# Local attention in a fused decoder layer: values two blocks behind the scores, with a fourth tile of probabilities

## Chip, core and metric

One core of a Trainium2 chip runs the whole layer as one program. The metric is device time in microseconds (us), the median over several executions; lower is better. The engines are called PE (TensorE, its products), PEld (TensorE's loading of weights), DVE (VectorE), ACT (ScalarE), POOL (GpSimd) and SP (SyncE, which here only issues DMAs).

## What is computed

The layer takes 1024 prompt tokens and 8 single decode tokens of width 1024 through one projection, three branches (a gated linear recurrence "a", local attention "s", attention into a memory of 256 tokens "c"), a gated merge, an output product, a norm, a gated feed-forward and a second norm. The change lies in the prompt's local attention: 16 query heads share 4 key/value heads of width 64, each block of 128 queries looks at its own block of keys and the one before, and a learned sink per head joins the softmax.

```python
def swa_prompt(q, k, v, sinks):
    nb = T // WINDOW                      # 8 blocks of 128
    s = jnp.einsum('bnqkgd,bnmkd->bnkgqm', qb, kband).astype(jnp.float32) * scale
    mask = (band[None] & real)[None, :, None, None]
    p = sink_softmax(s, mask, sinks).astype(v.dtype)
    o = jnp.einsum('bnkgqm,bnmkd->bnqkgd', p, vband)
    return o.reshape(B, T, Q_W)
```

The result of the branch is then multiplied by its own weight matrix and a gate and added to the merged sum, as those of the other two branches are: `merged = sum(gates[:, :, n] * (br @ w_branch[n]) ...)`.

## The kernel before

All values are float32. A float32 product is made of several products of a shortened form: every operand is split into a high part (a cast on ACT, line 79) and the rest (a subtraction on DVE, line 80), and `mm3` (lines 108 to 115) issues three products per pair, high by high, high by rest, rest by high.

The program goes through the projection (`project`), the memory attention (`mem_attention`), the local attention (`windows`), the last branch product, the output product, the feed-forward and the two norms. Intermediates that don't fit on the chip go to scratch in DRAM and come back.

The local attention is a stage of 32 blocks: 4 key/value heads (`kv`), and for each 8 blocks of 128 queries (`b`). A block has two steps.

- `win_scores` (lines 556 to 590): 8 products of queries with keys into two PSUM banks of tag "s" (lines 574 and 575, four pairs); on DVE the mask is added and the maximum taken (line 578, four times), which writes the tile of probabilities `bp`; POOL copies the sinks into that tile (line 568); ACT takes the exponentials in place with their sums (line 582, four times); DVE takes the reciprocals (line 583); the four heads are scaled in place, one on DVE, one on POOL (line 589) and two on ACT (line 587).
- `win_values` (lines 592 to 612): 8 transposes of the probabilities on PE (line 599, four per block of keys, into banks of tag "t"), each group of four cast and subtracted into a high and a low part (`bph` on ACT, `bpl` on DVE), then two products with the values per block of keys into the one bank of tag "o" (lines 604 and 605), and two rounds of copy (ACT, line 609), sum (DVE, line 610) and store to scratch by SP (line 612). The first block of each head has one block of keys: half the transposes and products.

The tile `bp` has 4 heads by 257 columns, 4112 bytes in each partition, and tag "p" has three of them. `win_load` (lines 538 to 554) brings keys, queries and values of the next head by SP; it is called at block 4.

Between the two steps stand pieces of other work: `fill(1)` takes one step of the generators of branches a and c (`branch` and `product`, lines 633 to 663). A step is one chunk of 258, 386 or 388 tokens by 128 outputs: 24 products on PE, sometimes preceded by a load and a split of the next weights. Memory attention and local attention share these 48 steps; `build` (lines 1317 to 1330) runs what is left, after the first loads of branch s.

What sets the order of the instructions: the Python text gives each instruction a place, and a scheduler at compile time then gives each engine its own fixed order. It takes instructions whose operands are expected to be ready first, by the text's order among those, and an allocation of a tile waits for the readers of the tile that held the buffer before. So an engine's order can differ from the text. On the chip each engine runs its list in order and waits on semaphores.

Of the kernel before, what the change touches and what calls it, by code (L numbers as in the profile page):

```python
# [10 lines left out]
F32 = mybir.dt.float32  # L11
# [7 lines left out]
P = 128  # L19
# [37 lines left out]
class Builder:  # L57
# [498 lines left out]
    def win_scores(self, kv, ops, b):  # L556

        nc = self.nc
        nk = 2 if b else 1
        n = nk * P  # L560
        k0 = max(b - 1, 0) * P
        msk = self.mask[:, 256 - n:]
        ks, q, _ = ops
        snk = self.nsnk[:, 4 * kv:4 * kv + 4]
        st = self.sm.tile([P, 12], F32, tag="bst", name=f"bst{kv}_{b}", bufs=4)
        p = self.ph.tile([P, 4, 257], F32, tag="p", name=f"bp{kv}_{b}", bufs=3)
        pg = [p[:, g, :n] for g in range(4)]
        nc.gpsimd.tensor_copy(p[:, :, n], snk)
        for pr in range(2):
            s = self.bank("s", f"bs{kv}_{b}_{pr}")  # L570
            for u in range(2):
                qq = q[2 * pr + u][:, b * P:(b + 1) * P]
                o = s[:, u * 256:u * 256 + n]
                nc.tensor.matmul(o, qq, ks[0][:, k0:k0 + n], start=True, stop=False)
                nc.tensor.matmul(o, qq, ks[1][:, k0:k0 + n], start=False, stop=True)
            for u in range(2):
                g = 2 * pr + u
                nc.vector.tensor_tensor_reduce(pg[g], s[:, u * 256:u * 256 + n], msk, 1.0, snk[:, g:g + 1],  # L578
                                               ALU.add, ALU.min, st[:, g:g + 1])
        for g in range(4):  # L580
            x = p[:, g, :n + 1]
            nc.scalar.activation(x, x, AF.Exp, bias=st[:, g:g + 1], scale=-1.0, accum_out=st[:, 4 + g:5 + g])  # L582
        nc.vector.reciprocal(st[:, 8:12], st[:, 4:8])
        for g in range(4):
            r = st[:, 8 + g:9 + g]
            if g % 2:
                nc.scalar.mul(pg[g], pg[g], r)
            else:
                (nc.gpsimd if g else nc.vector).tensor_scalar_mul(pg[g], pg[g], r)
        return pg  # L590
# [23 lines left out]
    def windows(self, fill):  # L614

        self.mask = self.ph.tile([P, 256], F32, tag="mask", name="mask", bufs=1)
        self.nc.sync.dma_start(self.mask, self.io["cst"][:, P:P + 256])
        nxt, last = self.win_load(0), None
        fill(2)
        for kv in range(4):  # L620
            ops = nxt
            for b in range(8):
                pg = self.win_scores(kv, ops, b)
                if last:
                    fill(1)
                    self.win_values(*last)
                last = kv, ops, b, pg
                if b == 4 and kv < 3:
                    nxt = self.win_load(kv + 1)
        fill(1)  # L630
        self.win_values(*last)

    def product(self, step, br, m, c, wb, gate):

# [866 lines left out]
```

## Time and profile before

| what | value |
|---|---|
| median of 3 runs | 1961.04 us (1960.61 to 1963.18) |
| the profiled execution | 1959.34 us, its span 1957.5 us |
| granted clock of TensorE, mean | 0.996 |
| busy share of the span | PE 98%, PEld 96%, DVE 70%, ACT 52%, POOL 6% |
| the local attention's first product of scores, last sum | 833.3 us, 1045.1 us from the span's start |

The profile is of one execution. Busy time of an engine is the time in which an instruction of it was running; matmuls are pipelined, their ends are modelled, and consecutive ones overlap in the records, so a start-to-start distance tells more of a product's cost than its duration. A line of waits reads "who <- what it waited for: us in total, times, longest". A line of a window reads: the stretch, its length, then for each engine the busy time and in brackets the number of instructions, then the granted clock, the share of DMA and GB/s.

### The profile page before, as it was taken

How to read it: one execution, taken by the hardware profiler on the slowest of the kernel's cores; microseconds unless marked ns; L12 is line 12 of the kernel's file. 1: busy time of each engine (PE TensorE's matmuls, PEld its weight loads, DVE VectorE, ACT ScalarE, POOL GpSimd, SP SyncE). 2: the span in 40 equal slices, each digit the busy share in tenths (PEclk: the TensorE clock that was granted, in tenths of full speed). 3: DMA queues.
4: the chain of work that ended last, by engine and by line, in shares of the span. 5: the costliest groups of instructions: out<-in, count | busy, mean ns of one | idle time of the engine just before them, and what ended most of it. 6: DMA issues, size and time to landing. Idle time of an engine off the chain costs nothing. (4 is left out here: it accounts for less than half of the span.)

```text
span 1957.5 us, 37935 instructions
## 1 busy us (share of the span) xinstructions
PE 1917.8 (98%) x14356; PEld 1888.3 (96%) x14356; DVE 1362.4 (70%) x2875; ACT 1014.3 (52%) x2198; POOL 124.9 (6%) x202
## 2 busy tenths in 40 slices
PE   8999999999999899999999999999999999999997
PEld 8999999999999899989999999999999999999997
DVE  8678987887876645379877457976565655747566
ACT  5465565464666545388775245643333333635445
POOL 0000010010000000012110000000000000402001
PEclk9999999999999899999999999999999999999999
DMA  7444455455323776567535341122222222846554
GB/s 230 149 165 155 163 175 181 128 200 174 133 95 120 238 248 210 155 170 221 154 85 166 104 144 42 49 71 97 78 87 87 87 82 71 284 127 187 154 154 143
DMA packets 172199, 281.92 MB, mean 144 GB/s; under 512 B 20864, under 2 KB 87504, under 8 KB 171984
## 3 DMA queue, kind: packets, MB, share of 16 engines
q1 hardware_dynamic: 168144, 267.87, 43.6%
q0 software_dynamic: 3872, 11.63, 1.8%
q8 instruction: 112, 1.84, 0.4%
q14 instruction: 71, 0.58, 0.1%
HBM read 214.64 MB, written 66.85 MB: 144 GB/s over the span
## 5 line engine op out<-in xcount | busy, mean ns | idle before, releaser
L1229 PE MATMUL dl<-gh,wd_l 128*128 128x388 f32 (+2 forms) x528 | 168.9, 320 | 2.1 <-DVE wd_l L80 2.1
L1227 PE MATMUL dl<-gh,wd_h 128*128 128x388 f32 (+2 forms) x528 | 169.0, 321 | 1.1 <-ACT gh L79 1.1
L1228 PE MATMUL dl<-gl,wd_h 128*128 128x388 f32 (+2 forms) x528 | 168.7, 320 | 0.0
L1229 PEld LDWEIGHTS dl<-gh,wd_l 128*128 128x128 f32 x528 | 99.7, 189 | 2.5 <-DVE wd_l L80 2.5
L1227 PEld LDWEIGHTS dl<-gh,wd_h 128*128 128x128 f32 x528 | 99.5, 189 | 1.3 <-ACT gh L79 1.3
L1228 PEld LDWEIGHTS dl<-gl,wd_h 128*128 128x128 f32 x528 | 99.7, 189 | 0.5 <-DVE gl L80 0.5
L1236 POOL DMA_DIRECT2D gl<-scr_f x66 | 35.6, 544 | 795.1 <-PE fb L1163 637.5
L79 ACT CAST u_2h<-us 128x512 fp32r<-128x512 f32 x48 | 29.8, 621 | 87.4 <-PE ub L293 41.6
L79 ACT CAST u_1h<-us 128x512 fp32r<-128x512 f32 x48 | 29.8, 621 | 85.5 <-PE uc L293 37.4
L582 ACT ACTIVATE bp<-bp,bst 128x257 f32<-128x257 f32 (+1 forms) x128 | 62.8, 493 | 17.4 <-DVE bst L578 17.4
L276 DVE TENSOR_TENSOR us<-ur,ur 128x512 f32<-128x512 f32 x96 | 66.0, 687 | 5.8 <-DMA ur<-win 3.1
L276 DVE TENSOR_TENSOR us<-us,ur 128x512 f32<-128x512 f32 x96 | 66.1, 689 | 2.3
L80 DVE TENSOR_TENSOR u_4l<-us,u_4h 128x512 fp32r<-128x512 f32 x48 | 33.8, 705 | 44.5 <-PE fb L1163 29.9
L292 PE MATMUL ub<-th,u_6h 128*128 128x258 f32 x224 | 63.5, 283 | 0.0
L293 PE MATMUL ub<-tl,u_4h 128*128 128x258 f32 x224 | 63.4, 283 | 0.0
L293 PE MATMUL ud<-tl,u_1h 128*128 128x258 f32 x224 | 63.4, 283 | 0.0
L293 PE MATMUL ub<-tl,u_6h 128*128 128x258 f32 x224 | 63.4, 283 | 0.0
L293 PE MATMUL ub<-tl,u_2h 128*128 128x258 f32 x224 | 63.4, 283 | 0.0
L292 PE MATMUL ud<-th,u_1h 128*128 128x258 f32 x224 | 63.4, 283 | 0.0
L292 PE MATMUL ub<-th,u_4h 128*128 128x258 f32 x224 | 63.3, 283 | 0.0
L292 PE MATMUL ub<-th,u_2h 128*128 128x258 f32 x224 | 63.3, 283 | 0.0
L294 PE MATMUL ub<-th,u_4l 128*128 128x258 f32 x224 | 63.3, 283 | 0.0
(2718 smaller groups left out, 7917.7 us busy)
## 6 DMA issues: line engine op xcount, KB each, us to landing
ur<-win SPq DMA_DIRECT2D x112, 256.0 KB, 3.2
ur<-wgu SPq DMA_DIRECT2D x80, 256.0 KB, 2.7
scr_f<-ft SPq DMA_DIRECT2D x40, 258.0 KB, 3.1
dck<-cmk SPq DMA_DIRECT2D x32, 256.0 KB, 3.5
dcv<-cmvT SPq DMA_DIRECT2D x32, 256.0 KB, 2.8
st<-scr_q SPq DMA_DIRECT2D x32, 256.0 KB, 6.3
scr_g<-za SPq DMA_DIRECT2D x10, 516.0 KB, 3.8
scr_g<-zb SPq DMA_DIRECT2D x10, 516.0 KB, 2.6
```

Source lines behind the costliest of these rows:

```text
L79: ins = self.nc.scalar.copy(hi, src).ins
L80: self.nc.vector.tensor_sub(lo, src, hi.bitcast(F32))
L276: nc.vector.tensor_add(src, a, b)
L292: mm(sh[:, w], xh, start=opens and k == 0, stop=False)
L293: mm(sh[:, w], xl, start=False, stop=False)
L294: self.last_mm = mm(sl[:, w], xh, start=False, stop=k == 3).ins
L582: nc.scalar.activation(x, x, AF.Exp, bias=st[:, g:g + 1], scale=-1.0, accum_out=st[:, 4 + g:5 + g])
L1227: nc.tensor.matmul(ps, sh, mh, start=k == 0, stop=False)
L1228: nc.tensor.matmul(ps, sh, ml, start=False, stop=False)
L1229: self.last_mm = nc.tensor.matmul(ps, sl, mh, start=False, stop=closes and k == NF - 1).ins
L1236: self.nc.gpsimd.dma_start(lo.bitcast(F32), self.scf[f][:, t0:t0 + n])
```

## The change

The values of a block are taken from a queue of blocks whose scores are issued; before, the queue held one block, now it holds two. In the text, the scores of block n+2 (counted through all 32) now stand ahead of the filling step and the values of block n; before, those of block n+1 did. At the end two blocks are left and are emptied with one filling step each, so that the number of filling steps in the stage stays 34. The tag of the probabilities gets a fourth tile. Nothing else is changed, and no arithmetic.

```diff
-        p = self.ph.tile([P, 4, 257], F32, tag="p", name=f"bp{kv}_{b}", bufs=3)
+        p = self.ph.tile([P, 4, 257], F32, tag="p", name=f"bp{kv}_{b}", bufs=4)
...
-        nxt, last = self.win_load(0), None
+        nxt, late = self.win_load(0), deque()
         fill(2)
         for kv in range(4):
             ops = nxt
             for b in range(8):
                 pg = self.win_scores(kv, ops, b)
-                if last:
+                late.append((kv, ops, b, pg))
+                if len(late) > 2:
                     fill(1)
-                    self.win_values(*last)
-                last = kv, ops, b, pg
+                    self.win_values(*late.popleft())
                 if b == 4 and kv < 3:
                     nxt = self.win_load(kv + 1)
-        fill(1)
-        self.win_values(*last)
+        while late:
+            fill(1)
+            self.win_values(*late.popleft())
```

## The prediction, made before the changed kernel ran

> **What bounds the kernel now.** I read the page first, then windows over the stage, then its waits, then single tiles and the timeline.
>
> ```profile
> span 1957.5 us, 37935 instructions
> ...
> PE 1917.8 (98%) x14356; PEld 1888.3 (96%) x14356; DVE 1362.4 (70%) x2875; ACT 1014.3 (52%) x2198; POOL 124.9 (6%) x202
> ```
>
> PE is busy for 98% of the span, so time goes only where PE stands still. The local attention runs from about 833 to 1046 us. Its windows (the whole in the last row):
>
> ```profile
> core 0: us, PE busy (x) PEld busy (x) DVE busy (x) ACT busy (x) POOL busy (x), PEclk, DMA share, GB/s
> 833.00:850.00 17.00, 17.00 (x122) 16.41 (x121) 10.53 (x45) 10.12 (x35) 2.28 (x5) 1.00 0.58 140
> 850.00:875.00 25.00, 23.59 (x151) 20.27 (x150) 22.55 (x74) 24.57 (x74) 6.22 (x11) 1.00 0.63 173
> 950.00:975.00 25.00, 24.65 (x169) 23.22 (x167) 20.75 (x63) 19.22 (x59) 5.85 (x8) 1.00 0.41 125
> 1050.00:1060.00 10.00, 9.17 (x51) 8.87 (x52) 8.59 (x18) 7.21 (x15) 0.00 (x0) 1.00 0.97 322
> 833.00:1046.00 213.00, 209.82 (x1350) 194.41 (x1349) 175.20 (x540) 162.94 (x488) 40.98 (x61) 1.00 0.55 150
> ```
>
> Over 213 us PE is idle for 213 − 209.82 = 3.2 us at full granted clock. DVE (82%) and ACT (76%) have room on the whole; only from 850 to 875 is ACT full (24.57 of 25), and there PE loses 25 − 23.59 = 1.41 us, against 0.35 in the steady stretch from 950. The change adds and removes no product, so 3.2 us of PE idle, 0.16% of the time, is about all that a better order could win by this measure.
>
> The Trainium skill (Perfetto Trace Analysis, Identifying the Most-Contended Engine) holds matmul busy time for a poor measure of headroom and asks for the busy share of weight loads. By it the stage has 213 − 194.41 = 18.6 us of room instead of 3.2. The trace agrees only in part:
>
> ```profile
> L605 PE MATMUL bo<-bpl,vs 128*128 128x512 f32 x60 | 24.3, 404 | 0.0
> ...
> L605 PEld LDWEIGHTS bo<-bpl,vs 128*128 128x128 f32 x60 | 11.3, 188 | 1.2 <-DVE bpl L80 0.3
> ```
>
> Here a load takes 188 ns and stands idle behind a longer stream, with PE never idle before it (0.0). I keep PE's own idle time as the measure and use PEld's as the outer bound.
>
> **What waits for the probabilities now.** The change can only shorten waits of the transposes (L599), the first readers of `bp`. The tile of transposed probabilities, `bt`, and the stage's waits:
>
> ```profile
> L599 PEld LDWEIGHTS bt<-ident,bp x240: 137/140/144, 844.8 to 1041.2; 128*128 128x128 f32 x120
> ...
> L599 PEldq EVENT_SEMAPHORE  x8: 51/51/51, 844.8 to 869.5; - x8
> ...
>   ACT bp L587: 0.7, 3
> ```
>
> ```profile
> PEld bo L604 <- ACT bph L79: 7.6, 25, 0.6
> ...
> PE bo L604 <- ACT bph L79: 1.5, 7, 0.4
> ...
> POOL bp L568 <- PE bt L599: 18.7, 15, 3.6
> ```
>
> In 240 transposes PE waited three times for `bp`, 0.7 us in all. The separate semaphore waits ahead of transposes end at 869.5. What PE's loads do wait for, 25 times and 7.6 us, is the cast `bph` (L79), which follows the transposes inside the same step: the distance between scores and values doesn't touch it. The wait for a free `bp` tile exists, but on POOL, busy for 41 of 213 us.
>
> Why is there no more? I counted instructions finished at 960.5 us, just after the transposes that start at 959.77.
>
> ```profile
> 0.00:960.50 960.50, 23.00 (x84) 15.88 (x84) 0.99 0.55 175
> ```
>
> ```profile
> 0.00:960.50 960.50, 21.48 (x147) 17.47 (x148) 0.99 0.55 175
> ```
>
> ```profile
> 0.00:960.50 960.50, 8.60 (x21) 21.08 (x21) 0.99 0.55 175
> ```
>
> These are lines L574, L599 and L589. 84 scores at four a block are blocks 0 to 20. 148 transposes are blocks 0 to 19 (eight each, four in blocks 0, 8 and 16). The 21 scalings on DVE and on POOL say that block 20's probabilities are finished. The timeline then shows PE, and POOL's scaling of block 20:
>
> ```profile
> 959.77 1.04 PE L599 MATMUL bt<-ident,bp 128*128 128x128 f32 x8
> 960.56 0.36 PE L574 MATMUL bs<-ks,st 128*128 128x256 f32 x1
> 960.77 0.28 PE L575 MATMUL bs<-ks,st 128*128 128x256 f32 x1
> 961.05 0.49 PE L604 MATMUL bo<-bph,vs 128*128 128x512 f32 x1
> ...
> 962.55 0.34 PE L113 MATMUL brc<-HL0h,wbc_h 128*128 128x386 f32 x1
> ...
> 967.01 1.04 PE L599 MATMUL bt<-ident,bp 128*128 128x128 f32 x8
> ```
>
> ```profile
> 959.22 1.08 POOL L589 TENSOR_SCALAR bp<-bp,bst 128x256 f32<-128x256 f32 x1 [4.92 <-DVE bst L583]
> ```
>
> Block 20's probabilities are done at 959.22 + 1.08 = 960.30 and transposed at 967.01: they lie ready for 6.7 us. And the scores at 960.56, between block 19's transposes and its values, are block 21's. The scheduled order is two blocks ahead already, although the text says one; the third tile is what it uses for that. The change makes it three ahead of something that already waits for nothing.
>
> **The change part by part.** The sequence of fills and values is the same 34 fills and 32 blocks in the same order; what moves is the scores, one block up against it.
>
> *Work.* Per block, 8 products, 4 reductions, 4 exponentials, the reciprocal, 4 scalings and POOL's copy are issued earlier, none added: 0 us of PE work. What hides the softmax is one period of about 7 us now and about two after; it was hidden before. Gain: the 0.7 us of waits for `bp`, next to come late being the cast before L604, which is there already.
>
> *The wait for a tile.* POOL's copy of block n+4, where n+3 stood, waits for the transposes of n; behind it on POOL stand scalings of earlier blocks. As the old wait did (18.7 us over 15), it falls into POOL's idle time: 0 us, and without that cover one copy's wait, up to 3.6 us (the longest).
>
> *Queues.* The two stores per block stay with the values. `win_load` moves up one fill and one block of values on SP. Its queries need two tiles that the last scores of the head release; the queue's own waits have it:
>
> ```profile
> SPq L612 <- DVE bob L610: 27.2, 13, 4.8
> ...
> SPq L550 <- PE bs L575: 1.8, 3, 1.2
> ```
>
> That wait is 1.8 us in three times, far below the 27.2 us in which the same queue stands for the stores, and the scores that end it move with the loads. Between 0 and ±1.8 us; I take 0, as the loads have one more block of other work before their values are read.
>
> *Start and end.* Three score blocks instead of two stand ahead of the first fill in the text; PE is full there (17.00 of 17). At the end the first product of branch s comes with PE idle for 10 − 9.17 = 0.83 us. It hangs on the last block's stores, whose place doesn't change: 0.
>
> *The tile.* 4112 bytes more per partition, over memory that earlier tiles hold. The tile's first writer and the first scores:
>
> ```profile
> L568 POOL COPY bp<-nsnk x32: 188/228/1377, 813.1 to 1022.1; 128x4 f32<-128x4 f32 x32
> ```
>
> ```profile
> L574 PE MATMUL bs<-ks,st x128: 218/282/368, 833.3 to 1030.3; 128*128 128x256 f32 x112, 128*128 128x128 f32 x16
> ```
>
> POOL writes the first tile at 813.1, 20 us ahead of the first scores; the fourth takes memory of the stage before, too, and that would have to come free 20 us later to be felt. Cost 0.
>
> **The sum.** 0.7 us from the profiled execution's 1959.34 (span 1957.5 plus 1.84 around it) gives 1958.6; the median stands 1.70 above that execution, so 1960.3. A change of 0.2%, 3.9 us, is about what a measurement of this kernel can tell from none; smaller counts as the same.
>
> **The rivals.**
>
> *Nothing moves*: the scheduler, already ahead of the text, finds the same order in the steady part. 1961.0. Against it: the fourth tile is a real freedom.
>
> *The early stretch relaxes.* In 850 to 875 ACT is full, and transposes follow their scalings closely. With more distance, PEld's idle there, 25 − 20.27 = 4.73, could fall to the steady stretch's 25 − 23.22 = 1.78: 2.95 us, 1958.1, still within 0.2%. Against it: ACT has the same work, and the score blocks that run ahead only load it sooner.
>
> *The repeated gaps close.* If the freer order put enough of another block's work before each L604, the 25 gaps would go: 7.6 + 1.5 = 9.1 us, 1951.9; it is faster by the bound from 3.9 of 9.1 on. Against it: the gap ends with a cast, not with a tile's release, and two scores are there to fill it. The Trainium skill (Perfetto Trace Analysis, Optimization Strategy) says that one gap repeating on the engine that should be full can mean too few buffers for the next tile; by that rule this would be the outcome. The rows speak against it, since the only engine that waits for a `bp` tile is POOL.
>
> *Slower: the filler leaves its place.* The scores between transposes and L604 (960.56 to 961.05, 0.49 us) cover the cast. If the freer order issues them before the transposes and no branch product comes in their stead, PE stands for 0.49 us a block: over the 0.2% from 8 blocks on, 28 × 0.49 = 13.7 us at the most with 28 full blocks; half of them gives 6.9 and 1967.9. For it: the fourth tile permits it. Against it: branch products follow at 962.55 and don't depend on the block.
>
> **How the numbers follow.** The forecast, 1960.3, has 0.41; nothing moves 0.05; the early stretch 0.14; the gaps 0.20; slower 0.20. So faster 0.20, same 0.41 + 0.05 + 0.14 = 0.60, slower 0.20. The range goes down to two thirds of the gaps, 1961.0 − 6.1 = 1954.9, and up to half the blocks, 1967.9; a third of the gaps' chance and half of slower's, some 0.17, lie outside. The likeliest case alone, with ±1.8 for SP's queue, is 1958.5 to 1962.1.
>
> **What would show it.** Right: scores of block n+3 between transposes and values of block n; probabilities ready some 13 us before they are transposed; the 0.7 us gone; the waits of L604 for `bph` near 9 us and PE's idle time in the stage near 3 us. Wrong: the waits of L604 below 5 us or above 13, PE's idle time in the stage changed by over 2 us, or a difference of several microseconds in stages that this change doesn't touch.

## The result, and the profile after

The changed kernel takes 1965.76 us in the median of 20 executions (1962.32 to 1970.67), the kernel before, run beside it, 1962.98 (1958.16 to 1966.20, 20 executions): a ratio of 1.0014, 95% interval 1.0007 to 1.0020. It is slower by about 2.8 us, less than the 0.2% that the prediction took as the least that can be told from none. With 20 executions of each kernel the interval is 0.07% to either side, so this smaller change is clear of none. The profiled execution of the changed kernel took 1962.32 us, 2.98 above that of before. The head of its page:

```profile
span 1960.5 us, 37929 instructions
...
PE 1918.2 (98%) x14356; PEld 1887.9 (96%) x14356; DVE 1363.0 (70%) x2875; ACT 1015.0 (52%) x2198; POOL 123.0 (6%) x202
```

PE has the same 14356 products, and its busy time grew by only 0.4 us. So 2.6 of the 3.0 us of span are standing time again. To place them, take the first scores of the local attention and the first product of branch s, which ends the stage. In the timeline of before (start, duration, instruction):

```profile
833.27 0.23 PE L574 MATMUL bs<-ks,st 128*128 128x128 f32 x1
...
1050.83 0.45 PE L113 MATMUL brs<-bsH,wbs_h 128*128 128x388 f32 x1 [1.01 <-ACT bsH L79]
```

and in that of after:

```profile
832.89 0.23 PE L574 MATMUL bs<-ks,st 128*128 128x128 f32 x1
...
1053.72 0.62 PE L113 MATMUL brs<-bsH,wbs_h 128*128 128x388 f32 x2 [1.01 <-ACT bsH L79]
```

The stage starts 0.38 us earlier and ends 2.89 us later: 217.56 us before, 220.83 after, 3.27 more. What comes after it is only shifted, by 2.9 to 3.0 us. Of the 3.27 us, 2.26 are PE's idle time in the stage (4.19 us before, 6.45 after); the other 1.01 are recorded as busy, with the same 1377 products at the same clock, and the records don't say why. The stage length is the number by which the experiments are compared below. The windows of after, at the places shown of before:

```profile
core 0: us, PE busy (x) PEld busy (x) DVE busy (x) ACT busy (x) POOL busy (x), PEclk, DMA share, GB/s
833.00:850.00 17.00, 17.00 (x120) 16.41 (x119) 11.12 (x48) 10.52 (x37) 2.71 (x4) 1.00 0.65 155
850.00:875.00 25.00, 23.18 (x147) 19.69 (x146) 20.83 (x70) 24.32 (x74) 6.20 (x10) 1.00 0.57 153
950.00:975.00 25.00, 23.82 (x155) 21.80 (x154) 20.23 (x61) 17.85 (x52) 3.88 (x7) 1.00 0.45 138
1050.00:1060.00 10.00, 8.99 (x57) 8.49 (x56) 7.77 (x16) 5.53 (x11) 0.00 (x0) 1.00 0.90 284
833.00:1046.00 213.00, 207.55 (x1332) 191.52 (x1331) 173.69 (x538) 162.96 (x486) 38.99 (x60) 1.00 0.54 150
```

PE's idle time over 213 us went from 3.18 to 213 − 207.55 = 5.45 us. The early stretch did not relax: its idle went from 1.41 to 1.82. PEld's idle there, by which the prediction priced that rival, went from 4.73 to 5.31. The steady stretch from 950, nearly full before, now loses 1.18 where it lost 0.35. The clock is 1.00 in both. The waits of after over the same 213 us (total, times, longest):

```profile
POOL bp L568 <- PE bt L599: 41.1, 19, 5.1
...
PEld bo L604 <- ACT bph L79: 9.4, 28, 0.9
...
PE bo L604 <- ACT bph L79: 2.0, 5, 0.7
...
PE bo L604 <- DVE bob L610: 1.0, 2, 0.8
...
PE bra L113 <- DVE M L642: 0.6, 1, 0.6
...
PE bs L574 <- DVE bst L578: 0.4, 1, 0.4
...
PE brc L113 <- ACT wbc_h L79: 0.3, 1, 0.3
...
PEld bt L599 <- ACT bp L587: 0.2, 1, 0.2
```

Five things are to be seen. The waits of the transposes for `bp` are 0.2 us on PEld, of 0.7 in all before: the gain that was forecast is there. The wait of the values for the cast `bph` grew from 7.6 + 1.5 = 9.1 to 9.4 + 2.0 = 11.4 us. Waits that PE's list of before did not have, for read-outs of PSUM by DVE, add 1.0 + 0.6 + 0.4 = 2.0 us: the bank of the output (`bob`, L610), that of a branch product (`M`, L642) and that of the scores (`bst`, L578). A cast of branch weights (`wbc_h`) comes too late for PE once. And POOL's wait for a tile more than doubled, 18.7 to 41.1 us; no wait of PE for POOL is among the rows. PE and PEld are two sequencers whose waits overlap, so rows of both can't be added to a loss of time. On PE alone, whose rows make up its idle time, the cast adds 0.5 us (1.5 to 2.0) and the read-outs 2.0.

PE's order is the one that was forecast. In the timeline of after, scores stand between the transposes and the values, and they do not cover the cast:

```profile
948.90 1.03 PE L599 MATMUL bt<-ident,bp 128*128 128x128 f32 x8
949.69 0.36 PE L574 MATMUL bs<-ks,st 128*128 128x256 f32 x1
...
951.09 0.50 PE L604 MATMUL bo<-bph,vs 128*128 128x512 f32 x1 [0.68 <-ACT bph L79]
```

What ACT did meanwhile:

```profile
948.26 0.62 ACT L79 CAST wbc_h<-wbc3r__12910 128x512 fp32r<-128x512 f32 x1 [0.41 <-DMA wbc3r__12910<-wbr]
948.79 0.90 ACT L587 ACTIVATE bp<-bp,bst 128x256 f32<-128x256 f32 x2
949.81 0.62 ACT L79 CAST wbc_h<-wbc3r__12916 128x512 fp32r<-128x512 f32 x1
950.46 0.59 ACT L79 CAST bph<-bt 128x512 fp32r<-128x512 f32 x1
```

The cast of the probabilities starts at 950.46 behind two rescalings of a younger block and two weight casts, the first of which had itself waited 0.41 us for its load, and PE stands for 0.68 us. The other kind of wait, on PE:

```profile
864.51 0.41 PE L605 MATMUL bo<-bpl,vs 128*128 128x512 f32 x1
...
867.62 0.47 PE L604 MATMUL bo<-bph,vs 128*128 128x512 f32 x1 [0.78 <-DVE bob L610]
```

and on ACT:

```profile
865.15 0.37 ACT L609 COPY bob<-bo 64x256 f32<-64x256 f32 x1
865.42 0.51 ACT L582 ACTIVATE bp<-bp,bst 128x257 f32<-128x257 f32 x1
865.83 0.19 ACT L582 ACTIVATION_READ_ACCUMULATOR bp<-bp,bst 128x1 f32 x1
866.04 0.59 ACT L79 CAST bph<-bt 128x512 fp32r<-128x512 f32 x1
866.65 0.37 ACT L609 COPY bob<-bo 64x256 f32<-64x256 f32 x1
```

The one output bank is written until 864.92. Its second half is copied only at 866.65, behind an exponential of a younger block and a cast; DVE's sum (L610) runs from 867.06 to 867.48, and the next values start at 867.62. Such places show where PE stood. That the lag causes them is not to be read from one trace; the experiments are for that.

### The profile page after: what moved, and what is told of

Its sections match the earlier page's. It is cut to its first block, busy times and chain, and to the rows that moved or that the text cites. A ratio compares the mean times of both kernels' runs of the same rounds, so it can differ in the third digit from the quotient of the medians.

```text
span 1960.5 us, 37929 instructions
## 1 busy us (share of the span) xinstructions
PE 1918.2 (98%) x14356; PEld 1887.9 (96%) x14356; DVE 1363.0 (70%) x2875; ACT 1015.0 (52%) x2198; POOL 123.0 (6%) x202
## 5 line engine op out<-in xcount | busy, mean ns | idle before, releaser
L294 PE MATMUL ud<-th,u_1l 128*128 128x258 f32 x224 | 63.3, 282 | 0.0
```

What stands on the lines that cost most here:

```text
L294: self.last_mm = mm(sl[:, w], xh, start=False, stop=k == 3).ins
```

## Experiments

18 kernels ran; each was timed over 11 or 12 executions beside 21 to 35 of the kernel before. The table has the stage as defined above, PE's idle time and ACT's busy time in it (from the windows cut at its two ends), and the ratio to before with its interval. Stage, idle and busy time are those of one profiled execution of each kernel. The ratio is the one on record; the quotient of the two medians differs from it by up to 0.0010 (fill_later: 0.9997 on record, 1.0006 by its medians), so smaller differences between ratios say little.

| kernel | stage us | PE idle us | ACT busy us | ratio (95% interval) |
|---|---|---|---|---|
| before | 217.56 | 4.19 | 164.65 | 1 |
| after | 220.83 | 6.45 | 165.41 | 1.0014 (1.0007 to 1.0020) |
| tile_only | 218.04 | 4.99 | 165.00 | 1.0003 (0.9994 to 1.0012) |
| order_only | 220.08 | 6.06 | 164.39 | 1.0016 (1.0007 to 1.0025) |
| fill_first | 219.10 | 6.08 | 165.82 | 1.0001 (0.9992 to 1.0010) |
| fill_later | 219.21 | 5.49 | 164.44 | 0.9997 (0.9989 to 1.0006) |
| before_bare | 219.03 | 6.07 | 149.36 | 1.0005 (0.9996 to 1.0014) |
| after_bare | 218.64 | 5.13 | 149.60 | 1.0008 (0.9999 to 1.0017) |
| before_ahead | 218.91 | 5.24 | 164.70 | 1.0008 (0.9999 to 1.0017) |
| after_ahead | 220.98 | 6.22 | 165.30 | 1.0018 (1.0009 to 1.0026) |
| before_pool | 222.60 | 8.00 | 139.53 | 1.0021 (1.0012 to 1.0031) |
| after_pool | 219.86 | 5.07 | 139.84 | 1.0020 (1.0009 to 1.0030) |
| lag1_fill_first | 219.07 | 6.52 | 165.31 | 1.0012 (1.0002 to 1.0021) |
| lag3 | 223.30 | 7.67 | 164.53 | 1.0030 (1.0020 to 1.0041) |
| before_swapscore | 211.66 | 4.97 | 163.34 | 1.0003 (0.9994 to 1.0012) |
| after_swapscore | 214.42 | 6.79 | 163.84 | 1.0016 (1.0007 to 1.0025) |
| before_load2 | 219.19 | 5.44 | 164.48 | 1.0002 (0.9993 to 1.0011) |
| after_load2 | 223.69 | 7.87 | 165.55 | 1.0027 (1.0018 to 1.0036) |
| before_swapout | 217.36 | 4.01 | 164.72 | 1.0000 (0.9991 to 1.0008) |
| after_swapout | 219.91 | 5.81 | 165.50 | 1.0013 (1.0004 to 1.0022) |

The two swapscore kernels have 43 products of the stage ahead of their first scores, so their stages compare only with each other.

**The tile or the order.** The first theory was late weights: the scores, a step higher in the text, go ahead of the loads of the branch weights, which then come late. Its rivals were the fourth tile and the distance itself. The kernel before with the fourth tile alone:

```diff
-        p = ... name=f"bp{kv}_{b}", bufs=3)
+        p = ... name=f"bp{kv}_{b}", bufs=4)
```

> Distance one as before, four tiles of probabilities. Measure: the stage from the first product of scores (L574) to the first product of branch s (before 217.6 us, after 220.8), and the whole time against the kernel before. Late weights (the scores, moved up against the fills, push the loads of branch weights behind stores that wait, and ACT's casts of them delay the cast of the probabilities): SP's order of weight loads is that of before, so stage 217.6 within 0.5 and ratio 1.000. Rival 'tile' (the fourth tile alone lets PE and ACT run ahead badly): stage near 220.8, ratio 1.0014. Rival 'distance' (probabilities held longer cost by themselves): stage 217.6.

It comes out as before, 1.0003. Its waits, over its stage:

```profile
PEld bo L604 <- ACT bph L79: 7.4, 26, 0.5
...
PE bo L604 <- ACT bph L79: 0.9, 5, 0.2
```

The repeated gaps stay: 8.3 us of 9.1. The tile alone doesn't cost measurable time, and it is no cure either. The prediction's rival by the Trainium skill (Perfetto Trace Analysis, Optimization Strategy: a repeated gap on the full engine may want more buffers) has its answer: these gaps don't end with the release of that buffer, and another one does not close them.

The changed kernel with three tiles:

```diff
-        p = ... name=f"bp{kv}_{b}", bufs=4)
+        p = ... name=f"bp{kv}_{b}", bufs=3)
```

> Distance two in the text as after, but three tiles as before. Late weights: the loads of weight tiles 1 to 4 of branch c stand behind 4 to 32 stores in SP's order, mostly no later than before (14, 24, 24, 24), so stage 217.6 to 219 us, ratio 1.000 to 1.0008. Rival 'tile': 217.6, ratio 1.000. Rival 'distance': near 220.8, ratio 1.0014, as the text's order is that of after.

It has the loss, 1.0016 and 220.08 us, so the order in the text carries it. Late weights expected the loss to be small here and missed. The loss lies elsewhere than in the changed kernel, though. PE's waits for the cast are as before (1.6 us, 1.5 before); what is new stands at the start of branch c's products:

```profile
PEld brc L115 <- DVE wbc_l L80: 1.5, 1, 1.5
PE brc L115 <- DVE wbc_l L80: 1.2, 1, 1.2
PE bo L604 <- DVE bob L610: 1.1, 1, 1.1
```

Two kernels move only the fills. In the changed kernel, the fill ahead of the scores:

```diff
             for b in range(8):
+                if len(late) > 1:
+                    fill(1)
                 pg = self.win_scores(kv, ops, b)
...
                 if len(late) > 2:
-                    fill(1)
                     self.win_values(*late.popleft())
```

> As after (values two blocks behind, four tiles), but the filling step stands ahead of the scores in the text, so that fills and scores stand to each other as before and only the values are later. Late weights: loads of weight tiles 2 to 4 stand behind 23 to 24 stores again (after: 25 to 34), only tile 1 is late (20), so stage 217.6 to 218.6 us, ratio 1.000 to 1.0006. Rivals 'tile' and 'distance': near 220.8, ratio 1.0014, since both the fourth tile and the distance are there.

And in the kernel before, each fill one block later:

```diff
                 if last:
-                    fill(1)
+                    if kv or b > 1:
+                        fill(1)
...
-        fill(1)
+        fill(2)
```

> As before (values one block behind, three tiles), but the first filling step between scores and values is left for the end, so that every fill comes one block of scores later. Late weights: loads of weight tiles 1 to 4 stand behind 22 to 35 stores, as late as after or later, so the stage is longer, 219.5 to 222 us, ratio 1.0010 to 1.0020, and ACT waits for landings of branch weights ahead of its casts. Rivals 'tile' and 'distance': 217.6, ratio 1.000, since neither the tile nor the distance changed.

fill_first is level with before in time (1.0001, and its interval ends at 1.0010), its stage only half-way (219.10). That is a miss for tile and for distance, both of which had it at 1.0014: the values are two blocks behind the scores here, with four tiles. fill_later should have been slower by late weights and is not (0.9997), though its stage is 1.65 us longer. So by here: order, not tile; late weights in doubt, and the distance is not enough by itself.

**Is it the preparation of the fills?** One pair leaves it out, in both kernels alike (branch c's loads and splits of weights after the first tile, and of its operands):

```diff
+            if br == "c":
+                self.act["c"] = self.act["a"]
-            if m == 0 and (c or br != "s"):
+            elif m == 0 and (c or br != "s"):
                 self.load_branch(br, c)
...
-                ops[m] = self.weights(...), gate
+                ops[m] = ops[0][0] if m and br == "c" else self.weights(...), gate
```

> The kernel before, with the preparation of the fill products of branch c left out: its seven later weight tiles are not loaded or split (the first tile's pairs are used again) and branch c's operands are not loaded or split (branch a's are used); PE has the same number and sizes of matmuls, the output is not the reference's. It is the base for the next kernel. Theory LATE PREPARATION (the loads, casts and subtractions of the fill products come later in the queues of SP, ScalarE and VectorE once the scores stand a block higher, and PE then waits for them or for what they hold up): the stage from the first scores to the first product of branch s, 217.6 us before, comes to 215.0-217.6, ratio 0.9990-1.0000, since 3.2 us of PE idle is all there is to win. Theory DISTANCE (the scores two blocks up put their exponentials and reductions ahead of the casts and stores of the older block, whatever the fills do): the same, 215.0-217.6. Theory CHANCE (each order of this stage comes out some us up or down, with no one mechanism): 215-220.

> The changed kernel with the same preparation left out as in before_bare. LATE PREPARATION: what made the change slower is gone, so its stage is within 0.7 us of before_bare's and its ratio within 0.0006 of it. DISTANCE: the 3.3 us by which the stage grew (217.6 to 220.8) stays: stage 2.3-4.0 us over before_bare's, ratio 0.0010-0.0020 over it. CHANCE: a difference of 1-3 us of either sign.

The pair is level: −0.39 us in the stage, 1.0005 against 1.0008. That is what late preparation said of the pair. But that doesn't show what the lag costs: the kernel before became worse, where every theory but chance had it at 217.6 us or less. Its waits for the cast, over its stage:

```profile
PEld bo L604 <- ACT bph L79: 10.0, 28, 1.8
...
PE bo L604 <- ACT bph L79: 3.7, 8, 1.6
```

13.7 us, with 15 us less work on ACT, where the kernel before has 9.1. The other pair leaves nothing out and prepares early: the raw weights two tiles ahead, each split two fills ahead.

```diff
+        def prepare(m):
+            ...
+            fetch(m)
+            ...
+            if br == "c":
+                fetch(m + 1)
+                fetch(m + 2)
...
             self.product(step, br, m, c, *ops[m])
+            if br == "c" and i < 22 and order[i + 2][1] == 0:
+                prepare(order[i + 2][0])
             yield
```

> Control. The kernel before, nothing left out, with branch c's raw weights loaded two tiles ahead and each tile split two fills ahead. Before the change the loads of tiles 2 to 4 were issued at 914-917 us and PE waited little for them: LATE PREPARATION: stage 217.0-218.2, ratio 0.9995-1.0005. DISTANCE: the same. CHANCE: 215-220 us, ratio 0.999-1.001.

> The changed kernel, nothing left out, with branch c's raw weights loaded two tiles ahead and each tile split two fills ahead: in SP's order 10, 14, 22 and 26 stores then stand ahead of the loads of tiles 1 to 4, where the changed kernel has 20, 26, 33 and 34 and the kernel before 14, 24, 24 and 24. LATE PREPARATION: the loss goes: stage 217.0-218.5, ratio 0.9995-1.0006, no wait of ScalarE for a weight DMA, waits of L604 for bph under 10 us in sum. DISTANCE: nothing is gained, since the scores stand where they stood: stage 220.0-221.5, ratio 1.0010-1.0020, waits of L604 for bph near 11 us. CHANCE: 216-222.

The loss stays, 220.98 us and 1.0018, as distance said of time and stage; late preparation had 217.0 to 218.5 and falls as the whole cause. In the waits it was the other way round: distance had L604 wait near 11 us for the cast, and it waits 7.7 + 0.9 = 8.6, as little as in the control (8.8). The control is itself longer than both theories had it (218.91 us). In after_ahead no product of branch c waits for its weights; PE waits for DVE's read-outs instead, 3.4 us, of which the control has 0.7:

```profile
PE bo L604 <- DVE bob L610: 1.8, 4, 0.8
...
PE bs L574 <- DVE bst L578: 1.0, 2, 0.6
...
PE bra L113 <- DVE M L642: 0.6, 1, 0.6
```

**Is it ACT's queue, and does it grow with the lag?** In a pair ACT's two rescalings per block go to POOL:

```diff
-            if g % 2:
-                nc.scalar.mul(pg[g], pg[g], r)
-            else:
-                (nc.gpsimd if g else nc.vector).tensor_scalar_mul(pg[g], pg[g], r)
+            (nc.gpsimd if g else nc.vector).tensor_scalar_mul(pg[g], pg[g], r)
```

> The kernel before, with the two rescalings per block that ScalarE does (L587, 56 x 505 ns + 8 x 394 ns = 31 us with the short ones, measured 28.3 us in the stage) given to GpSimd, which then does three of a block's four (3 x 1.05 = 3.2 us a block, under the 6.65 us that a block takes). It is the base for the next kernel. Theory ORDER STEP (each step by which the scores stand higher in the text against fills and values lets their reductions and activations stand ahead, in VectorE's and ScalarE's in-order queues, of the casts and read-outs that PE's values and fill products wait for): the stage, 217.6 us before, stays at 216.0-218.0, ratio 0.9990-1.0003. Theory CHANCE (each order of the stage draws its waits anew, around 218.5 with about 1 us of spread, and the order of the changed kernel is a poor draw): 217.0-220.0.

> The changed kernel with the same rescalings given to GpSimd. ORDER STEP, if ScalarE's queue carries it: with 28 us of ScalarE's 163 us gone the casts come sooner, the stage is within 1.0 us of before_pool's, ratio within 0.0006 of it; if it is VectorE's queue instead, the 3.3 us stay: stage 2.3-4.0 us over before_pool's. CHANCE: a difference anywhere from -2 to +2 us.

ACT has 25 us less to do, and the kernel before gets worse (222.60 us), which neither theory had. The three scalings in a row on POOL come late, and transposes wait for them (over the stage of before_pool; its lines stand three lower from there on, so L596 is the transposes and L586 the scalings):

```profile
PEld bt L596 <- POOL bp L586: 3.6, 7, 0.8
...
PE bt L596 <- POOL bp L586: 1.8, 5, 0.6
```

With the longer lag these fall to 1.5 and 0.6 us, and the stage is 2.74 us shorter: where the probabilities do come late, the longer lag shortens the stage, more than any of the theories had. In time the pair is level, 1.0021 and 1.0020. As a test of ACT's queue it is spoilt by this second effect.

Half a step against the change, in the kernel before, and one step further with it (the same four tiles):

```diff
             for b in range(8):
+                if last:
+                    fill(1)
                 pg = self.win_scores(kv, ops, b)
                 if last:
-                    fill(1)
                     self.win_values(*last)
```

> The kernel before, with each fill ahead of the scores in the text instead of behind them: half a step further from the change than the kernel before. The steps so far: 0 (before) 217.6 us, 1/2 (fill_first) 219.1, 1 (the changed kernel) 220.8. ORDER STEP: 1.6 us less than before: 215.5-217.0, ratio 0.9988-0.9997. CHANCE: 217.3-220.0, ratio 0.9998-1.0012.

```diff
-                if len(late) > 2:
+                if len(late) > 3:
```

> The changed kernel with the values three blocks behind the scores, with the same four tiles: one step more. ORDER STEP: 3.3 us more than the changed kernel: 222.5-225.0, ratio 1.0025-1.0040. CHANCE: 217.3-220.5, ratio 1.0000-1.0015.

The third block of lag costs again, 2.47 us more in the stage: 223.30 us, 1.0030, within what order step said. Its waits for the cast, over its stage:

```profile
PEld bo L604 <- ACT bph L79: 9.3, 23, 1.9
PE bo L604 <- ACT bph L79: 3.9, 8, 1.7
...
PEld bs L574 <- DVE bst L578: 1.3, 3, 0.7
```

Not all of the 2.47 us is waiting. 0.7 us after its longest wait for the cast, 1.74 us, the granted clock fell to one half for 3.41 us:

```profile
932.25:935.66 3.41, 3.41 (x15) 3.13 (x15) 1.69 (x6) 0.90 (x5) 0.00 (x0) 0.50 0.64 145
```

Half of 3.41 us, an estimated 1.7, is lost there; PE's idle time grew by 1.22 (6.45 to 7.67).

But half a step the other way is no gain, it costs too (219.07 us, 1.0012). The kernel before stands near the best place, and order step as a straight line falls. The waits for the cast don't follow the lag either: the longest of all kernels are those of lag1_fill_first, with the short lag:

```profile
PEld bo L604 <- ACT bph L79: 10.6, 27, 1.9
...
PE bo L604 <- ACT bph L79: 4.2, 7, 1.7
```

lag1_fill_first and fill_first are also a pair: the same edit, the fill ahead of the scores, in the kernel before and in the changed one. Here no cost of the longer lag shows: stage 219.07 and 219.10 us, ratio 1.0012 and 1.0001. PE's waits for the cast fall from 4.2 to 1.7 us, and its waits for read-outs rise from none to 1.2.

**The lag, or the one order that it gives?** That was left open: any rearrangement of this stage might cost something. So the same harmless edit was made to both kernels, three times more, with the fill where it was. The pairs of heads in the other order:

```diff
-        for pr in range(2):
+        for pr in (1, 0):
             s = self.bank("s", f"bs{kv}_{b}_{pr}")
```

> The kernel before, with the two pairs of heads of a block's scores computed in the other order (second pair first): the same instructions, only the order that comes out of it differs. With the next kernel it is one of three pairs in which the same harmless edit is made to the kernel before and to the changed kernel. Theory LAG (the stage is longer because the scores stand a block higher, in whatever order): stage 216.5-219.0, ratio 0.9995-1.0006. Theory DRAW (rearranging this stage costs some us whatever is rearranged, because the order of the kernel before is an unusually close fit; the lag is one such rearrangement): stage 218-221, ratio 1.0005-1.0020.

> The changed kernel with the same edit as before_swapscore. LAG: stage 2.0-4.5 us over that of before_swapscore, ratio 0.0010-0.0022 over its ratio. DRAW: stage 218-222, the difference between the two from -2 to +2 us, ratio within 0.0010 of it.

The next head's operands loaded at another block:

```diff
-                if b == 4 and kv < 3:
+                if b == 2 and kv < 3:
                     nxt = self.win_load(kv + 1)
```

> The kernel before, with the next kv's operands loaded after block 2 instead of after block 4: the same instructions in another order. LAG: stage 216.5-219.0, ratio 0.9995-1.0006. DRAW: stage 218-221, ratio 1.0005-1.0020.

> The changed kernel with the same edit as before_load2. LAG: stage 2.0-4.5 us over that of before_load2, ratio 0.0010-0.0022 over its ratio. DRAW: stage 218-222, the difference from -2 to +2 us, ratio within 0.0010 of it.

The halves of the output read out in the other order, which leaves PE's order as it is:

```diff
-        for i in range(2):
+        for i in (1, 0):
             ob = self.ph.tile([64, 256], F32, tag="ob", ...)
```

> The kernel before, with the two halves of a block's output read out of PSUM in the other order (second half first): TensorE's order of instructions stays the same to the last one, only ScalarE's, VectorE's and SP's orders differ. Theory LAG (the stage is longer because the scores stand a block higher, in whatever order): stage 216.5-219.0, ratio 0.9995-1.0006. Theory DRAW (any rearrangement of this stage costs some us, the order before being a close fit): stage 218-221, ratio 1.0005-1.0020.

> The changed kernel with the same edit as before_swapout; TensorE's order is that of the changed kernel. LAG: stage 2.0-4.5 us over that of before_swapout, ratio 0.0010-0.0022 over its ratio. DRAW: the difference from -2 to +2 us, ratio within 0.0010 of it.

Each time the edited kernel before is level with the unedited one (1.0003, 1.0002, 1.0000), and each time the lag adds to it: 2.76, 4.50 and 2.55 us in the stage, 0.0013, 0.0025 and 0.0013 in the ratio, 2.7, 4.6 and 2.1 us between the medians. Draw had the differences within 2 us, and misses. It isn't quite wrong: before_load2's stage, 219.19 us, lies in its range and above that of lag, and fill_later, before_ahead and lag1_fill_first, which have the short lag, are 1.35 to 1.65 us longer than before.

The 4.50 us of load2 need a second look. after_load2 waits for a cast of branch weights,

```profile
PE brc L113 <- ACT wbc_h L79: 2.0, 1, 2.0
```

and 1.4 us after that wait its clock is at one half, again for 3.41 us (911.83 to 915.24 us), an estimated 1.7 us. So late weights do cost in this pair, and without the half clock some 2.8 us would be left, as in the other pairs.

The last pair shows the kind of wait that the lag adds there. Over the stage of before_swapout:

```profile
PEld bo L604 <- ACT bph L79: 7.5, 25, 0.5
...
PE bo L604 <- ACT bph L79: 1.3, 6, 0.4
```

and of after_swapout:

```profile
PEld bo L604 <- ACT bph L79: 8.7, 27, 0.9
PE bo L604 <- ACT bph L79: 1.5, 3, 0.7
PE bo L604 <- DVE bob L610: 1.0, 2, 0.8
...
PE bra L113 <- DVE M L642: 0.6, 1, 0.6
...
PE bs L574 <- DVE bst L578: 0.4, 1, 0.4
```

These are the rows of the changed kernel, where the pair of before has none of the last three.

**What stands and what is open.** The pairs side by side, short lag and long lag. The waits are those of PE alone, from their rows over each stage: of L604 for the cast `bph`, and for DVE's read-outs (`bob`, `bst` and L642's `M`).

| pair | stage, us more | ratio | for the cast, us | for read-outs, us |
|---|---|---|---|---|
| the change itself | 3.27 | 1 to 1.0014 | 1.5 to 2.0 | 0 to 2.0 |
| three tiles (before, order_only) | 2.52 | 1 to 1.0016 | 1.5 to 1.6 | 0 to 1.3 |
| ahead | 2.07 | 1.0008 to 1.0018 | 1.3 to 0.9 | 0.7 to 3.4 |
| swapscore | 2.76 | 1.0003 to 1.0016 | 1.6 to 2.9 | 0.6 to 1.0 |
| load2 | 4.50 | 1.0002 to 1.0027 | 1.2 to 1.2 | 0.2 to 0.9 |
| swapout | 2.55 | 1.0000 to 1.0013 | 1.3 to 1.5 | 0 to 2.0 |
| fill first | 0.03 | 1.0012 to 1.0001 | 4.2 to 1.7 | 0 to 1.2 |
| bare | −0.39 | 1.0005 to 1.0008 | 3.7 to 1.8 | 0 to 1.6 |
| pool | −2.74 | 1.0021 to 1.0020 | 2.4 to 0.8 | 0.2 to 0.2 |

With the fill behind the scores and all work on its engines (the first six rows) the longer lag lengthens the stage by 2.07 to 4.50 us and raises the ratio by 0.0010 to 0.0025, with three tiles as with four; a third block of lag raises it further. With the fill ahead of the scores, with branch c's preparation left out, or with the rescalings on POOL no cost of it shows. So the loss belongs to the lag together with the order around it. The read-out waits rise with the lag in all pairs but pool. Those for the cast fall by 1.6 to 2.5 us in the three pairs without a loss, and in the others they rise or fall by less.

In five of the six pairs with a loss (all but that with three tiles) the cast of the probabilities comes later: the 60 casts and 60 groups of four transposes, paired in order, show it starting 0.91 us after the transposes end in before and 1.04 in after, and 0.96 and 1.25, 1.01 and 1.06, 1.05 and 1.15, 0.90 and 1.03 in the pairs ahead, swapscore, load2 and swapout; in lag3 it is 1.37. But a later cast is no measure of the loss: it starts 0.85 us after them in order_only, which loses, and 1.41 and 1.47 in lag1_fill_first and fill_first. That ACT's and DVE's instructions for younger blocks hold up casts and read-outs for older ones is how I read this, and it is not shown. Added up from the traces, between transposes and casts ACT was busy with exponentials and rescalings of younger blocks for 33.7 us in before and 35.1 in after, and with casts of weights and operands of the branches for 9.0 and 11.7: the latter grew more. Which of the two queues carries the loss was not settled, and no pair takes work off DVE alone. No version ran faster than the kernel before beyond its interval.

## Why the prediction was wrong

- **What bounds the kernel**: right. PE's work is the same, the 3.27 us lie in the stage that the change touches, and 2.26 of them are PE's idle time.
- **The scheduled order**: right. The scores of another block stand between transposes and values, and the probabilities lie ready twice as long: block 20's, by the count of the prediction, from 958.1 to 970.8 us, 12.7 us instead of 6.7. The scores at 949.69 in the timeline above are block 20's, and the transposes ahead of them block 17's.
- **The gain**: right in kind. Waits for `bp` fell from 0.7 to 0.2 us. There was no more to win, since they were nearly hidden.
- **Work, the step that failed.** "4 reductions, 4 exponentials, the reciprocal, 4 scalings and POOL's copy are issued earlier, none added: 0 us", and of the cast, "the distance between scores and values doesn't touch it". The instructions were counted, and what their new place does to other waits of PE was put at nothing without a reason. Measured on PE itself, the waits for DVE's read-outs went from none to 2.0 us and those for the cast from 1.5 to 2.0, against 0.2 gained on PE (0.5 with PEld's), and PE's idle time grew by 2.27. With PEld's rows the waits for the cast went from 9.1 to 11.4 us. So the term of the sum that should have stood at some 2 us or more stood at 0, and the sign came out wrong with it. That the moved instructions stand in the way in ACT's and DVE's queues is my reading of it; the cause in that sense stays open. The prediction had the thought, as an argument against a rival: "the score blocks that run ahead only load it sooner". It gave that no price.
- **The wait for a tile**: right. POOL's wait rose to 41.1 us, and PE waits for POOL in no row.
- **The tile**: right, by tile_only, 1.0003 (0.9994 to 1.0012).
- **Queues**: only `win_load` was considered, at 0 ± 1.8. The loads of the branch weights on SP fell behind too (tile 1's at 900 us instead of 881, tile 3's at 943 instead of 915, by their issue). Bringing them forward did not remove the loss.
- **Start and end**: right. PE is full at the start (17.00 of 17), and the wait before branch s is 1.01 us in both.
- **The rivals**: slower came true by another mechanism. Scores stood between transposes and values as before, and other waits grew. That the time still lies within the stated range is owed to the range, which the rivals set, and not to the forecast. The early stretch did not relax (idle 1.41 to 1.82), and the gaps before L604 did not close.
- **What would show it wrong**: PE's idle time changed by 2.27 us, just over the 2 us named there, and the waits of L604 for `bph` were 11.4 us, neither near 9 nor above 13. The 0.20 for slower was too small a share: the gain was bounded by 0.7 us, while the same engines released 9.1 us of other waits.

## What to carry to other kernels

Before a deeper lag between two steps is made, compare what its consumer waits for with what the moved producer's engines release: here the consumer waited 0.7 us for the producer, and the same engines released 9.1 us of other waits on the bounding engine. A step that is ready long ahead is not free to be put still further ahead: its instructions change places with casts and read-outs that are needed now, and that had a price in six of the nine pairs here. To tell an effect from the luck of a list-scheduled order, make the same harmless edit in both versions, and include one that could make the effect go away: three such pairs had the loss again, and a fourth, with the fill ahead of the scores, had none.

## What the runs showed of the hardware

Less work on an engine that is not the bound did not help PE: with 15 us less on ACT and 17 us less on DVE (before_bare) the stage was 1.5 us longer, at a ratio of 1.0005 whose interval includes 1. With 25 us of ACT's work moved to POOL (before_pool) it was 5.0 us longer. A scaling of 128 by 256 elements that takes ACT 0.505 us took POOL 1.05 us, so that three in a row, 3.2 us, were already seen by PE, in blocks that take about 6.65 us each.

A short wait of PE can be followed by a stretch at half the granted clock. In lag3 and after_load2 PE stood for 1.74 and 1.96 us, and 0.7 and 1.4 us later the clock was at one half for 3.41 us; products of 388 columns then started 0.32 us apart in after_load2, and 0.18 us right after. It does not always follow: PE stood for 1.71 us in the stage of lag1_fill_first and for 1.65 in that of after_swapscore, and the clock stayed at 1.00.
